# FFN chains in a two-layer hybrid decoder: where the addition, the scaled copy, the convolution taps and the gelu or gate product are issued

## The chip, the cores and the metric

The kernel runs on one core of one Trainium2 chip. The metric is the device time of one execution in microseconds, the median of three runs; it is compared with the same kernel after the change.

## The reference

A decoder trunk of two layers works on x of shape (1, 512, 1024) in float32. Layer 0 mixes tokens by dilated windowed attention, layer 1 by a gated recurrent block. Each is followed by a gated feed-forward block (FFN), and every block is wrapped in RMS norms. The change touches the FFN alone:

```python
D_FF = 3 * D_MODEL            # 3072

def causal_dwconv(x, w, b):   # K = 3 taps along the sequence
    xp = jnp.pad(x, ((0, 0), (K - 1, 0), (0, 0)))
    out = b
    for k in range(K):
        out = out + xp[:, k:k + S] * w[k]
    return out

def conv_ffn(x, w_up, conv_w, conv_b, w_down):
    u = causal_dwconv(x @ w_up, conv_w, conv_b)
    g, v = u[..., :D_FF], u[..., D_FF:]
    return (jax.nn.gelu(g, approximate=True) * v) @ w_down
```

## The kernel before

**Arithmetic.** Every matrix product is made of three passes of float32r matmuls: each operand is split into a high part (`whi`, a copy on ScalarE, line 149) and a low part (`wlo`, what the copy left out, a subtraction on VectorE, line 150). A weight of one unit can be multiplied only when both engines have split it.

**Chunks and chains.** The 6144 columns of `w_up` come in 12 chunks j of 256 gate columns (half 0) and 256 value columns (half 1). Chunks 0 to 2 are multiplied in the plain way. For chunks 3 to 11 (`SEVEN`) each half is a *chain*: seven products of 128x128x256 blocks in place of eight. The chain's steps are numbered 1 to 7 and collect in two PSUM banks: the *top* bank `y[0]` (output features 0 to 127) and the *bottom* bank `y[1]`. There are 18 chains in each layer; we call them c0 to c17, an even number for half 0 (gate) and an odd one for half 1 (value).

**Slots.** `seven` lays the steps on a line of slots, ten for each chain (`CYCLE`). Within a chain's ten, `AT` puts step 1 in slot 0, step 5 in 1, step 2 in 2, step 6 in 4, step 3 in 5, step 7 in 8, and step 4 in slot 3 of the next ten. Slots 6, 7 and in some chains 9 hold fill: quarters of the last plain chunk at first, then products of `w_down`'s first columns into four PSUM banks `acc` (line 412). Slots that hold nothing are skipped.

**What a slot issues.** `slot` emits the matmuls of its step, then counts down the list `due` and runs what has reached its turn, then `tick` splits one further unit of weights (line 149 on ScalarE, line 150 on VectorE). `later(0, f)` called from a step runs f at the end of the same slot, `later(1, f)` at the end of the next one; called from the list itself, f runs one slot later than that. Each engine works through its own instructions strictly in the order of issue, as written by this code; nothing rearranges them later.

**After the steps.** ScalarE copies three partial products out of PSUM (`part`, line 1032) before a later step adds to the same place. After step 3 comes the top's chain of work: the addition on VectorE (line 1036), the scaled copy on ScalarE with the middle tap's weight and the bias (line 773), the two other taps on VectorE, which read the bank once more (line 777), and at last either gelu on ScalarE (line 795, even chains) or the gate product on VectorE (line 799, odd chains). After step 7 VectorE adds a partial product to the bottom bank (line 1041), and step 4 adds to that bank in turn, so TensorE waits for line 1041. After step 4 the bottom has its scaled copy, taps, and gelu or gate product.

The waiting list stands in these lines:

```python
    def later(n, f):
        due.append([n, f])

    def slot(emit, length=1):
        emit()
        for d in list(due):
            d[0] -= 1
            if d[0] < 0:
                due.remove(d)
                d[1]()
        tick(length)
```

`begin` issues the scaled copy when it is called, puts the taps on the list with `later(0, taps)`, and returns gelu or the gate product for `finish` to put on the list.

Of the kernel before, what the change touches and what calls it, by code (L numbers as in the profile page):

```python
# [83 lines left out]
def kernel(  # L84
# [45 lines left out]
    def psum(s="ps"):  # L130
        return pp.tile([P, 512], F32, tag="ps", name=nm(s))
# [60 lines left out]
    def free_slots(n):  # L192

        end = CYCLE * n
        free = [CYCLE * c + r for c in range(n) for r in ((6, 7, 9) if c < 3 or c > 8 else (6, 7))][2:] + [end, end + 1]
        assert not {CYCLE * c + a for c in range(n) for a in AT.values()} & set(free)
        return free
# [149 lines left out]
    def take(i, j):  # L347
        while (i, j) not in units:
            before = state["live"]
            pump(1)  # L350
            assert before != state["live"], (i, j, state)
        return units[i, j]

    def done(n=2):
        state["live"] -= n
# [6 lines left out]
# [11 lines that stand above are left out]
# [37 lines left out]
    def mm3(dst, l, r, start, stop):  # L410
        for n, (a, b) in enumerate(PASSES):
            mm(dst, l[a], r[b], start=start and n == 0, stop=stop and n == 2)  # L412
# [569 lines left out]
    def rights(hT, T):  # L982

        def block(kr, n):
            return lambda h, k: hT[h][:, 4 * kr + k, n * 256 : n * 256 + 256]

        def turn(n):
            return lambda h, k: T[n][h][k // 2][:, k % 2]

        return {  # L990
            1: block(0, 0), 2: block(1, 0), 3: block(1, 1), 5: turn(0), 6: turn(1), 7: turn(2), 4: turn(3),
        }

    def quarters(i, m, hT, finish):
        ps = []

        def quarter(n):
            W = take(i, m)
            if not n:
                ps.append(psum())  # L1000
            for k in (2 * n, 2 * n + 1):
                mm3(ps[0], [w[k // 4][:, k % 4, :] for w in W], [h[:, k, :] for h in hT], k == 0, k == KD - 1)
            if n % 2:
                done(1)
            if n == 3:
                later(1, lambda: finish(ps[0]))

        return [lambda n=n: quarter(n) for n in range(4)]

    def chain(right, top, bottom):  # L1010

        i = chunk()
        y, t = {}, []

        def step(n):
            W = take(i, LEFT[n][0])
            b, at = {1: (1, 0), 6: (1, 0), 7: (1, 0), 4: (1, 0), 5: (0, 256), 3: (0, 256), 2: (0, 0)}[n]
            if b not in y:
                y[b] = psum()
            dst = y[b][:, at : at + 256]  # L1020
            for k in range(4):
                for q, (wa, ha) in enumerate(PASSES):
                    mm(  # L1023
                        dst, W[wa][0][:, k, :], right[n](ha, k), start=n in (1, 5) and k == q == 0,
                        stop=k == 3 and q == 2, skip_group_check=True,
                    )
            done(1)
            if n == 1:
                t.extend(gen(s="part") for _ in range(2))
            if n in (1, 5, 6):  # L1030
                to = {1: t[0][:, 0:256], 6: t[0][:, 256:512], 5: t[1][:, 0:256]}[n]
                later(1, lambda: nc.scalar.activation(to, dst, AF.Copy))  # L1032
            elif n == 3:

                def upper():
                    nc.vector.tensor_tensor(y[0], y[0], t[0], op=ALU.add)  # L1036
                    top(y[0])

                later(1, upper)
            elif n == 7:  # L1040
                later(1, lambda: nc.vector.tensor_tensor(y[1][:, 256:512], dst, t[1][:, 0:256], op=ALU.add))  # L1041
            elif n == 4:
                later(1, lambda: bottom(y[1]))

        return lambda n: lambda: step(n)

    def seven(hT, T, begin, last, prep):

        right = rights(hT, T)
        i0, acc, ends_at = state["next"], {}, CYCLE * 2 * len(SEVEN)  # L1050

        def finish(b, ps, j, minus=False):
            later(1, begin(b, ps, j, minus, True))

        def ends(j, half):
            return lambda ps: finish(2 * half, ps, j), lambda ps: finish(2 * half + 1, ps, j, True)

        def rows(k, pair):
            W, A = take(i0, ("rows", k)), take(i0, ("act", k))
            for t in pair:  # L1060
                if t not in acc:
                    acc[t] = psum("acc")
                mm3(acc[t], [a[0][:, t * P : (t + 1) * P] for a in A], [w[0] for w in W], not k, False)
            if pair[-1] == 3:
                done(2)

        fill = []
        for m in range(2):
            fill += quarters(last, m, hT, lambda ps, m=m: finish(2 + m, ps, SEVEN[0] - 1))
        fill += [lambda k=k, p=p: rows(k, p) for k in range(REST[0]) for p in ((0, 1), (2, 3))]  # L1070
        steps = {}
        n = 0
        for j in SEVEN:
            for half in range(2):
                f = chain(right, *ends(j, half))
                steps.update((CYCLE * n + AT[p], f(p)) for p in AT)
                n += 1
        free = free_slots(n)
        assert len(free) == len(fill)
        steps.update(zip(free, fill))  # L1080
        state["even"] = True
        for m in range(max(steps) + 1):
            if m == ends_at - 2:
                prep()
            if m in steps:
                slot(steps[m])
        while due:
            slot(lambda: None)
        done(2)
        state["even"] = False  # L1090
        return acc
# [626 lines left out]
```

## Time and profile before

| what | value |
|---|---|
| median of three runs (lowest to highest) | 1433.02 us (1432.54 to 1433.49) |
| profiled execution: its own time | 1433.17 us |
| profiled execution: span of the core | 1431.3 us |
| TensorE busy | 1407.8 us, 98% of the span |
| VectorE busy | 1124.2 us, 79% |
| ScalarE busy | 789.8 us, 55% |
| granted TensorE clock, mean | 0.999 |

The profile names engines PE (TensorE matmul), PEld (TensorE weight load), DVE (VectorE), ACT (ScalarE), POOL (GpSimd) and SP (SyncE). A row of the timeline begins with start and duration in microseconds; idle time of the engine just before it, and what ended that, stand in brackets at its end. The 18 chains of layer 0 lie between 549 and 805 us of the span, those of layer 1 between 1096 and 1352 us.

### The profile page before, as it was taken

Reading aid. Unit: us, or ns where it says so; the run is one execution under the profiler, and the core shown is the slowest. Engines: PE = TensorE matmul, PEld = TensorE weight load, DVE = VectorE, ACT = ScalarE, POOL = GpSimd, SP = SyncE. Lnnn points to the kernel's source line nnn. Section 1 sums busy time; section 2 is a strip of 40 time slices with the busy share of each in tenths; the row PEclk is TensorE's granted clock in tenths of the full one; section 3 lists DMA queues with packets and bytes.
Section 4 is the critical chain, followed back from the end, with each engine's and each line's share of the span. In section 5 each row is a group of like instructions: output and inputs, shape, how many; then the busy total and the mean of one; then the engine's idle time right before and its main releaser. Section 6 shows DMA issues by size and latency. Waiting matters only on the chain.

```text
span 1431.3 us, 23653 instructions
## 1 busy us (share of the span) xinstructions
PE 1407.8 (98%) x8741; PEld 1266.5 (88%) x8741; DVE 1124.2 (79%) x2201; ACT 789.8 (55%) x1646; POOL 225.3 (16%) x344
## 2 busy tenths in 40 slices
PE   9999999999999999999999999999999999999998
PEld 7888999999998888899999889888898989999886
DVE  6676898787855988888887758779789888888843
ACT  7343555363636555556656545588455656665641
POOL 0341333130400102121110001000102112111000
PEclk9999999999999999999999999999999999999999
DMA  7653455564756446576663632432345657574411
GB/s 225 180 145 106 131 166 153 169 181 141 196 165 220 164 131 127 112 155 149 132 151 86 221 118 89 133 118 89 118 151 107 154 112 157 135 151 117 165 64 60
DMA packets 171886, 201.93 MB, mean 141 GB/s; under 512 B 10561, under 2 KB 141081, under 8 KB 171513
## 3 DMA queue, kind: packets, MB, share of 16 engines
q1 hardware_dynamic: 123064, 153.34, 33.7%
q0 software_dynamic: 47856, 46.02, 17.6%
q8 instruction: 69, 1.13, 0.3%
q10 hardware_dynamic: 848, 1.05, 0.2%
q14 instruction: 49, 0.39, 0.1%
HBM read 181.41 MB, written 18.96 MB: 140 GB/s over the span
## 4 chain that ended last, share of the span: by engine, by line
PE 78%; DVE 12%; ACT 6%; issue 3%; DMA 1%; POOL 0%; DVEq 0%; SPq 0%; ACTq 0%
PE ps L1023 32%; PE acc L412 24%; PE ps L412 10%; PE v L1216 7%; DVE wlo L150 3%; DVE u L777 3%; ACT whi L149 2%; PE v L1154 1%; DVE xb L1521 1%; PE O L1428 1%; PE S L1362 1%; PE S L1310 1%; DVE T L150 1%; DVE u L799 1%; DVE B L939 1%
## 5 line engine op out<-in xcount | busy, mean ns | idle before, releaser
L150 DVE TENSOR_TENSOR wlo<-raw,whi 128x512 fp32r<-128x512 f32 x620 | 410.0, 687 | 130.5 <-ACT whi L149 125.8
L149 ACT ACTIVATE whi<-raw 128x512 fp32r<-128x512 f32 x620 | 366.6, 625 | 173.4 <-PE ps L1023 52.0
L1023 PE MATMUL ps<-T,whi 128*128 128x256 f32 x1664 | 305.3, 283 | 14.2 <-DVE ps L1041 10.5
L412 PE MATMUL ps<-hT,whi 128*128 128x512 f32 (+1 forms) x1088 | 288.0, 353 | 0.0
L1023 PEld LDWEIGHTS ps<-T,whi 128*128 128x128 f32 x1664 | 258.4, 189 | 21.7 <-DVE ps L1041 13.9
L1023 PE MATMUL ps<-T,wlo 128*128 128x256 f32 x832 | 232.9, 280 | 0.0
L1023 PE MATMUL ps<-hT,whi 128*128 128x256 f32 x1248 | 230.5, 283 | 0.0
L412 PEld LDWEIGHTS ps<-hT,whi 128*128 128x128 f32 x1088 | 190.8, 189 | 26.4
L1023 PEld LDWEIGHTS ps<-hT,whi 128*128 128x128 f32 x1248 | 195.7, 191 | 2.6
L412 PE MATMUL ps<-hT,wlo 128*128 128x512 f32 (+1 forms) x544 | 191.3, 352 | 0.0
L1023 PE MATMUL ps<-hT,wlo 128*128 128x256 f32 x624 | 176.4, 283 | 0.0
L186 POOL DMA_DIRECT2D raw<-in_ffn_w_up_dram x72 | 92.8, 1318 | 438.1 <-DVE wlo L150 294.5
L1023 PEld LDWEIGHTS ps<-T,wlo 128*128 128x128 f32 x832 | 158.1, 190 | 0.0
L412 PE MATMUL acc<-whi,ahi 128*128 128x512 f32 x352 | 137.6, 391 | 0.0
L412 PE MATMUL acc<-whi,alo 128*128 128x512 f32 x352 | 137.2, 390 | 0.2
L412 PE MATMUL acc<-wlo,ahi 128*128 128x512 f32 x352 | 137.0, 389 | 0.0
L1023 PEld LDWEIGHTS ps<-hT,wlo 128*128 128x128 f32 x624 | 119.3, 191 | 0.0
L412 PEld LDWEIGHTS ps<-hT,wlo 128*128 128x128 f32 x544 | 102.9, 189 | 14.0
L1216 PE MATMUL v<-whi,hT 128*128 128x512 f32 x320 | 106.5, 396 | 0.0
L777 DVE SCALAR_TENSOR_TENSOR u<-ps,cols,u 128x511 f32<-128x511 f32 x120 | 89.6, 747 | 5.0 <-ACT u L773 2.9
L773 ACT ACTIVATE u<-ps,cols 128x512 f32<-128x512 f32 x60 | 46.4, 774 | 76.8 <-DVE ps L1036 66.5
L1032 ACT ACTIVATE part<-ps 128x256 f32<-128x256 f32 x156 | 58.3, 374 | 50.0 <-PE ps L1023 49.1
(206 smaller groups left out, 2145.2 us busy)
## 6 DMA issues: line engine op xcount, KB each, us to landing
raw<-in_ffn_w_up_dram SPq DMA_DIRECT2D x48, 1024.0 KB
raw<-in_attn_w_qkv_dram SPq DMA_DIRECT2D x67, 512.0 KB
raw<-in_ffn_w_up_dram POOLq DMA_DIRECT2D x72, 256.0 KB, 5.7
raw<-in_ffn_w_down_dram SPq DMA_DIRECT2D x14, 1024.0 KB
dw<-in_ffn_w_down_dram SPq DMA_DIRECT2D x40, 256.0 KB
raw<-in_lru_w_in_dram SPq DMA_DIRECT2D x8, 1024.0 KB
turned<-T POOLq DMA_DIRECT2D x26, 256.0 KB, 2.6
ft<-turned POOLq DMA_DIRECT2D x104, 64.0 KB, 4.9
```

Source lines behind the costliest of these rows:

```text
L149: nc.scalar.activation(hi, raw, AF.Copy)
L150: nc.vector.tensor_tensor(lo, raw, hi.bitcast(F32), op=ALU.subtract)
L186: nc.gpsimd.dma_start(to, src, accum_op=ALU.add)
L412: mm(dst, l[a], r[b], start=start and n == 0, stop=stop and n == 2)
L773: nc.scalar.activation(u, ps, AF.Identity, scale=own[:, j : j + 1], bias=cc[:, 48 + j : 49 + j])
L777: nc.vector.scalar_tensor_tensor(u[:, d:], ps[:, : S - d], wc, u[:, d:], op0=ALU.mult, op1=ALU.add)
L799: nc.vector.tensor_tensor(g, g, u, op=ALU.mult)
L939: tt(o, hi.bitcast(F32), lo.bitcast(F32), op=ALU.add)
L1023: mm(dst, W[wa][0][:, k, :], right[n](ha, k), start=n in (1, 5) and k == q == 0, stop=k == 3 and q == 2, skip_group_check=True,)
L1032: later(1, lambda: nc.scalar.activation(to, dst, AF.Copy))
L1154: mm(banks[t], hT[a][:, k, t * P : (t + 1) * P], W[b][k % 2][:, 0, :], start=u == n == 0, stop=u == 3 and n == 5,)
L1216: mm(bank, hT[a][:, k, t * P : (t + 1) * P], W[b][k % 2][:, 0, :], start=(k, a, b) == (0, 0, 0), stop=(k, a, b) == (KD - 1, 1, 0),)
```

## The change

For the top bank, `ends` now puts the call of `finish` on the list with `later(0, ...)`, so the scaled copy is issued one slot after the addition in place of the same slot, and the taps one slot later too. `finish` puts gelu or the gate product three slots behind the scaled copy in place of two; this holds for tops, for bottoms, and for the two quarters of the last plain chunk, which end in `finish` too. No instruction is added or removed, and the matmuls keep their order.

```diff
         def finish(b, ps, j, minus=False):
-            later(1, begin(b, ps, j, minus, True))
+            later(2, begin(b, ps, j, minus, True))

         def ends(j, half):
-            return lambda ps: finish(2 * half, ps, j), lambda ps: finish(2 * half + 1, ps, j, True)
+            return (
+                lambda ps: later(0, lambda: finish(2 * half, ps, j)),
+                lambda ps: finish(2 * half + 1, ps, j, True),
+            )
```

How this moves instructions is seen in three pieces, all of layer 0. Names carry the number that the program gives a tile (`ps_7361` is chain c6's top bank, `ps_7335` its bottom bank); between the two programs these numbers shift by one or more without meaning.

First, VectorE in the even chain c6, from the split before the top's addition to the bottom's addition, before:

```order
L799 TENSOR_TENSOR u_7267<-u_7267,u_7426 128x512
L1036 TENSOR_TENSOR ps_7361<-ps_7361,part_7348 128x512
L150 TENSOR_TENSOR wlo_7462<-raw_7039,whi_7461 128x512
L777 SCALAR_TENSOR_TENSOR u_7459<-ps_7361,cols_1202,u_7459 128x511
L777 SCALAR_TENSOR_TENSOR u_7459<-ps_7361,cols_1202,u_7459 128x510
L150 TENSOR_TENSOR wlo_7474<-raw_7200,whi_7473 128x512
L150 TENSOR_TENSOR wlo_7491<-raw_7200,whi_7490 128x512
L1041 TENSOR_TENSOR ps_7335<-ps_7335,part_7349 128x256
```

And the same place after the change:

```order
L1036 TENSOR_TENSOR ps_7360<-ps_7360,part_7347 128x512
L150 TENSOR_TENSOR wlo_7459<-raw_7037,whi_7458 128x512
L799 TENSOR_TENSOR u_7267<-u_7267,u_7426 128x512
L150 TENSOR_TENSOR wlo_7472<-raw_7199,whi_7471 128x512
L777 SCALAR_TENSOR_TENSOR u_7469<-ps_7360,cols_1202,u_7469 128x511
L777 SCALAR_TENSOR_TENSOR u_7469<-ps_7360,cols_1202,u_7469 128x510
L150 TENSOR_TENSOR wlo_7490<-raw_7199,whi_7489 128x512
L1041 TENSOR_TENSOR ps_7334<-ps_7334,part_7348 128x256
```

The addition L1036 moved ahead of a gate product, and the taps moved behind one more split; L1041 keeps its place in the row.

Second, ScalarE at the same place in c6, from the split before the scaled copy to the copy of the next chain's step 1, before:

```order
L149 ACTIVATE whi_7447<-raw_7039 128x512
L773 ACTIVATE u_7459<-ps_7361,cols_1206 128x512
L149 ACTIVATE whi_7461<-raw_7039 128x512
L149 ACTIVATE whi_7473<-raw_7200 128x512
L795 ACTIVATE u_7459<-u_7459 128x512
L149 ACTIVATE whi_7490<-raw_7200 128x512
L149 ACTIVATE whi_7510<-raw_7039 128x512
L1032 ACTIVATE part_7507<-ps_7494 128x256
```

And after the change:

```order
L149 ACTIVATE whi_7447<-raw_7037 128x512
L149 ACTIVATE whi_7458<-raw_7037 128x512
L773 ACTIVATE u_7469<-ps_7360,cols_1206 128x512
L149 ACTIVATE whi_7471<-raw_7199 128x512
L149 ACTIVATE whi_7489<-raw_7199 128x512
L149 ACTIVATE whi_7509<-raw_7037 128x512
L795 ACTIVATE u_7469<-u_7469 128x512
L1032 ACTIVATE part_7506<-ps_7493 128x256
```

One split moved ahead of the scaled copy L773, and gelu L795 moved behind two more splits, to stand right in front of the `part` copy.

Third, VectorE in the chain c2, one of the first, where the fill is still quarters of the last plain chunk. Before:

```order
L799 TENSOR_TENSOR u_6603<-u_6603,u_6778 128x512
L1036 TENSOR_TENSOR ps_6711<-ps_6711,part_6702 128x512
L150 TENSOR_TENSOR wlo_6815<-raw_6572,whi_6814 128x512
L777 SCALAR_TENSOR_TENSOR u_6812<-ps_6711,cols_1202,u_6812 128x511
L777 SCALAR_TENSOR_TENSOR u_6812<-ps_6711,cols_1202,u_6812 128x510
L150 TENSOR_TENSOR wlo_6827<-raw_6572,whi_6826 128x512
L150 TENSOR_TENSOR wlo_6844<-raw_6443,whi_6843 128x512
L210 TENSOR_TENSOR raw_6572<-raw_6572 128x4x128
L1041 TENSOR_TENSOR ps_6689<-ps_6689,part_6703 128x256
```

And after the change:

```order
L1036 TENSOR_TENSOR ps_6711<-ps_6711,part_6701 128x512
L150 TENSOR_TENSOR wlo_6812<-raw_6572,whi_6811 128x512
L799 TENSOR_TENSOR u_6603<-u_6603,u_6778 128x512
L150 TENSOR_TENSOR wlo_6825<-raw_6572,whi_6824 128x512
L777 SCALAR_TENSOR_TENSOR u_6822<-ps_6711,cols_1202,u_6822 128x511
L777 SCALAR_TENSOR_TENSOR u_6822<-ps_6711,cols_1202,u_6822 128x510
L150 TENSOR_TENSOR wlo_6843<-raw_6443,whi_6842 128x512
L210 TENSOR_TENSOR raw_6572<-raw_6572 128x4x128
L1041 TENSOR_TENSOR ps_6688<-ps_6688,part_6702 128x256
```

Again the addition moved ahead of the gate product, and the taps behind one more split. In c3, which follows, two gate products that stood ahead of L1041 now stand behind it.

## The prediction

> **What bounds the kernel now.** I read the page first, then who waited for whom on TensorE in the two FFN stretches, then the timeline of each wait found, then VectorE and ScalarE ahead of it. The page's first part says that TensorE sets the time:
>
> ```profile
> PE 1407.8 (98%) x8741; PEld 1266.5 (88%) x8741; DVE 1124.2 (79%) x2201; ACT 789.8 (55%) x1646; POOL 225.3 (16%) x344
> ```
>
> VectorE and ScalarE matter only where TensorE waits for them. In the chains of layer 0 (549 to 805 us) the view of waits has just two rows for TensorE, with total, count and longest; for layer 1 (1096 to 1352 us) it gives the same two rows with the same numbers:
>
> ```profile
> PE ps L1023 <- DVE ps L1041: 4.7, 5, 1.6
> PE ps L1023 <- ACT part L1032: 1.8, 1, 1.8
> ```
>
> So a layer has five stalls on the bottom's addition (L1041) and one on a `part` copy. That one stands at the start of chain c0, ahead of the first instruction that the change moves, and stays. Four of the five in TensorE's timeline (the missing one is at 620.88 us); the bracket holds the idle time:
>
> ```profile
> 592.92 0.50 PE L1023 MATMUL ps<-T,whi 128*128 128x256 f32 x2 [1.60 <-DVE ps L1041]
> ...
> 607.30 0.51 PE L1023 MATMUL ps<-T,whi 128*128 128x256 f32 x2 [1.38 <-DVE ps L1041]
> ...
> 647.26 0.50 PE L1023 MATMUL ps<-T,whi 128*128 128x256 f32 x2 [0.58 <-DVE ps L1041]
> ...
> 673.66 0.50 PE L1023 MATMUL ps<-T,whi 128*128 128x256 f32 x2 [0.58 <-DVE ps L1041]
> ```
>
> Each is step 4 of a chain: at 592.92 that of c2, then c3, (c4), c6 and c8. How long TensorE needs where nothing holds it is seen in the chain of waits (start, duration, what):
>
> ```profile
> 592.92 4.55 PE ps L1023 x36
> ...
> 712.03 8.58 PE ps L1023 x72
> 720.61 2.75 PE acc L412 x12
> 723.36 1.42 PE ps L1023 x12
> ...
> 799.59 1.70 PE ps L1023 x12
> ```
>
> A step of 12 matmuls takes 8.58 / 6 = 1.43 us; six steps, two fills and step 7 make a cycle of 8.58 + 2.75 + 1.42 = 12.75 us. After a stall three steps take 4.55 where 3 x 1.43 = 4.29 would do: each stall costs 0.26 us more than its idle time.
>
> Why is L1041 late? VectorE in c6, then ScalarE in the same stretch:
>
> ```profile
> 639.44 0.68 DVE L150 TENSOR_TENSOR wlo<-raw,whi 128x512 fp32r<-128x512 f32 x1
> 640.04 0.68 DVE L799 TENSOR_TENSOR u<-u,u 128x512 f32<-128x512 f32 x1
> 640.64 0.69 DVE L1036 TENSOR_TENSOR ps<-ps,part 128x512 f32<-128x512 f32 x1
> 642.76 0.69 DVE L150 TENSOR_TENSOR wlo<-raw,whi 128x512 fp32r<-128x512 f32 x1 [1.42 <-ACT whi L149]
> 643.37 1.53 DVE L777 SCALAR_TENSOR_TENSOR u<-ps,cols,u 128x511 f32<-128x511 f32 x2
> 644.81 0.68 DVE L150 TENSOR_TENSOR wlo<-raw,whi 128x512 fp32r<-128x512 f32 x1
> 646.17 0.69 DVE L150 TENSOR_TENSOR wlo<-raw,whi 128x512 fp32r<-128x512 f32 x1 [0.68 <-ACT whi L149]
> 646.78 0.43 DVE L1041 TENSOR_TENSOR ps<-ps,part 128x256 f32<-128x256 f32 x1
> ```
>
> ```profile
> 641.43 0.78 ACT L773 ACTIVATE u<-ps,cols 128x512 f32<-128x512 f32 x1 [2.59 <-DVE ps L1036]
> 642.11 1.14 ACT L149 ACTIVATE whi<-raw 128x512 fp32r<-128x512 f32 x2
> 644.99 0.63 ACT L795 ACTIVATE u<-u 128x512 f32<-128x512 f32 x1 [1.74 <-DVE u L777]
> 645.53 1.13 ACT L149 ACTIVATE whi<-raw 128x512 fp32r<-128x512 f32 x2
> 646.57 0.36 ACT L1032 ACTIVATE part<-ps 128x256 f32<-128x256 f32 x1
> ```
>
> The two engines block each other. ScalarE stands 2.59 us in front of the scaled copy, which needs the addition, with splits queued behind it; VectorE then waits 1.42 us for such a split. ScalarE next stands 1.74 us in front of gelu, which needs the taps, and VectorE waits 0.68 us for the split behind it. Those 2.10 us in the row ahead of L1041 are more than the 0.58 us by which L1041 is late.
>
> **The change part by part.** Nothing is added or removed; no DMA and no matmul is moved against its own engine's order. What changes is which instruction stands at the head of a queue when its input is not there.
>
> *Even chain, c6.* Instructions on VectorE start 0.60 to 0.61 us apart (639.44, 640.04, 640.64), two taps take 1.44 (643.37 to 644.81). In the new row the addition takes the gate product's place at 640.04. The scaled copy starts 0.79 later (641.43 less 640.64), at 640.83; the split behind it 0.68 later, at 641.51, and its `wlo` 0.65 later (642.76 less 642.11), at 642.16. Meanwhile VectorE has a `wlo` whose split is now ahead of the scaled copy, in ScalarE's 2.59 idle us (640.64), and the gate product (641.24 to 641.84): it idles 0.32, not 1.42. Then `wlo` 642.16, taps 642.77, `wlo` 644.21 (its split followed at 642.1), L1041 at 644.82, over at 645.25. TensorE asks at 647.26 - 0.58 = 646.68. Margin 1.4 us, with nothing gained earlier; c8 has the same rows.
>
> *c2.* VectorE, with ScalarE's copy behind it:
>
> ```profile
> 585.16 0.69 DVE L799 TENSOR_TENSOR u<-u,u 128x512 f32<-128x512 f32 x1
> 585.76 0.69 DVE L1036 TENSOR_TENSOR ps<-ps,part 128x512 f32<-128x512 f32 x1
> 587.82 0.69 DVE L150 TENSOR_TENSOR wlo<-raw,whi 128x512 fp32r<-128x512 f32 x1 [1.36 <-ACT whi L149]
> ...
> 592.45 0.43 DVE L1041 TENSOR_TENSOR ps<-ps,part 128x256 f32<-128x256 f32 x1
> ```
>
> ```profile
> 586.49 0.78 ACT L773 ACTIVATE u<-ps,cols 128x512 f32<-128x512 f32 x1 [4.97 <-DVE ps L1036]
> ```
>
> New: addition 585.16, `wlo` 585.76, gate product 586.36, copy 585.89 (0.73 behind the addition), split 586.57, its `wlo` 587.22, taps 587.83, `wlo` 589.27, L210 589.87, L1041 590.48 to 590.91. TensorE asks at 592.92 - 1.60 = 591.32: margin 0.4 us, the smallest; what c0 and c1 save in the same way would come on top.
>
> *c3.* Two gate products leave the row ahead of L1041:
>
> ```profile
> 601.39 0.69 DVE L150 TENSOR_TENSOR wlo<-raw,whi 128x512 fp32r<-128x512 f32 x1 [1.43 <-ACT whi L149]
> ...
> 606.82 0.43 DVE L1041 TENSOR_TENSOR ps<-ps,part 128x256 f32<-128x256 f32 x1
> ```
>
> L1041 was at 606.82; c2's gain of 1.97, two gate products (1.2) and the idle 1.43 (the first split now stands ahead of the copy, and the quarter's taps come before the top's) put it at 602.2 to 602.7. TensorE, 1.86 us earlier by c2's stall, asks at 607.30 - 1.38 - 1.86 = 604.06: margin 1.4. The two gate products then delay c4 by 1.2, and c4 saves 1.8 of its own idle time as c6 does; its margin comes out near 1.3.
>
> *Odd chains.* They have no stall; there the gate product moves from ahead of L1041 to behind it, 0.6 us in favour. In c17 L1041 came so late that step 4 took 1.70 us (at 799.59) in place of 1.42: 0.28 comes back.
>
> *What gets later.* The top's bank is emptied one split (0.6 us) later in the row. By the Trainium skill (PSUM — Partial Sum Buffer, Summary: rules for kernel authors) a bank should be emptied promptly, PSUM being tight; that speaks against the change. The trace has no TensorE wait for L777 at all, so here I set it at nothing; it is a rival below. Gelu and gate products come up to three units later, and their products are read in fills and in the down projection, chains later.
>
> *Sum.* Per layer 4.7 (the idle time of the five stalls, by the row of the waits; the four that are shown make 4.14 of it) + 5 x 0.26 + 0.28 = 6.3; both layers 12.6 us. A second way: from 592.92 to 673.66 lie 80.74 us and six cycles of 12.75 = 76.5, so 4.24, with the first 1.60 and 0.28 makes 6.12, both layers 12.2 us. I take 12.4. The profiled execution's own time is 1433.17, 0.15 above the median of 1433.02; from the median, **1420.6 us**. Bounds: the 0.26 terms don't come back (10.0 us saved, 1423), or the whole first sum does, on a run at the low end of those shown (1432.54 - 12.6 = 1419.9).
>
> **The rivals.** *A, half the gain.* c2's 0.4 us is thin: if ScalarE's splits there are held by something else than the scaled copy, c2 and c3 keep stalling and only the three small stalls go: 2 x (4.7 - 1.60 - 1.38 + 3 x 0.26) = 5.0 us, 1428. For it: ScalarE's 4.97 us at c2's copy say that VectorE was far behind by its own work. Against: in those 4.97 us ScalarE could have made the splits that VectorE then waits for. Chance 0.12.
>
> *B, slower: gelu in front of the `part` copy.* In even chains the copy of the next chain's step 1 now stands right behind gelu, and gelu waits for the taps. Step 6 adds where that copy reads. In c6 the new taps end at 644.21, gelu and copy (0.63 + 0.36) at 645.3; step 6 is one step behind step 4, at 646.68 + 1.43 = 648.1. It decides once taps end after 647.1, 2.9 us later than worked out. If TensorE then waited 1 us in each of the 18 even chains, 18 x 1.26 = 22.7 lost against 12.4 gained: 1443. For it: gelu did wait 1.74 us for the taps in c6. Against: the margin. Chance 0.04.
>
> *C, slower: the bank.* A chain that takes over a top's bank waits for its taps. c6's taps end at 644.81, and c7 already writes both its banks:
>
> ```profile
> 643.66 0.40 PE L1023 MATMUL ps<-T,whi 128*128 128x256 f32 x2
> ```
>
> So the taker is c8 at the earliest, a cycle later, and a move of 0.6 us does not reach it. If it did, one step of 1.43 in 36 chains would give 51 us, about 1472. This is what the skill's rule above would lead to; chance 0.01.
>
> *D, no change.* TensorE runs into another wait of the same size at the same step, a split that is itself paced by a buffer TensorE frees. Against it: no TensorE wait for a split stands in the two rows above. About 1433; chance 0.03.
>
> **How the numbers follow.** The forecast has 0.80: 1419.5 to 1423. With A at 0.12 near 1428 and values between (c2's stall left: 1420.6 + 2 x 1.86 = 1424), the range 1419 to 1427 leaves out most of A and B, C and D, under 2 in 10. A measurement of this kernel can tell about 0.2%, 2.9 us, from no change. Forecast and A are faster by more: 0.92; D 0.03 within; slower B and C, 0.05.
>
> **What would show it.** Right: TensorE's waits for L1041 in the two stretches gone, cycles c3 to c8 12.75 us long, VectorE's wait ahead of the split behind the scaled copy near 0.3 us in even chains, ScalarE's waits at L773 well below the 2.59 and 4.97 us of before. c2 alone still stalling means the margin there was misjudged. Wrong: waits for L1032 in even chains (B), for L777 (C), or for L150 (D).

## The result

| what | before | after |
|---|---|---|
| median of three runs (lowest to highest) | 1433.02 us (1432.54 to 1433.49) | 1420.84 us (1420.83 to 1420.89) |
| ratio after / before, 95% interval | | 0.9915 [0.9893, 0.9938] |
| profiled execution: own time, span | 1433.17, 1431.3 us | 1420.89, 1419.1 us |
| granted TensorE clock, mean | 0.999 | 0.998 |

The changed kernel is 12.2 us faster; 1420.6 was forecast.

### The profile page after: what moved, and what is told of

It reads as the page before. It is cut to its first block, busy times and chain, and to the rows that moved or that the text cites. A ratio compares the mean times of both kernels' runs of the same rounds, so it can differ in the third digit from the quotient of the medians.

```text
span 1419.1 us, 23634 instructions
## 1 busy us (share of the span) xinstructions
PE 1406.0 (99%) x8741; PEld 1267.6 (89%) x8741; DVE 1125.1 (79%) x2201; ACT 800.6 (56%) x1646; POOL 225.8 (16%) x344
## 4 chain that ended last, share of the span: by engine, by line
PE 83%; DVE 9%; ACT 5%; issue 1%; DMA 0%; POOL 0%; DVEq 0%; ACTq 0%
PE ps L1023 35%; PE acc L412 25%; PE ps L412 11%; PE v L1219 7%; DVE wlo L150 3%; DVE u L777 2%; PE v L1157 1%; DVE xb L1524 1%; PE O L1431 1%; PE S L1365 1%; ACT whi L149 1%; PE S L1313 1%; DVE T L150 1%; DVE B L939 1%; ACT sig L1545 1%
## 5 line engine op out<-in xcount | busy, mean ns | idle before, releaser
L149 ACT ACTIVATE whi<-raw 128x512 fp32r<-128x512 f32 x620 | 371.0, 626 | 189.3 <-PE ps L1023 76.3
L1023 PE MATMUL ps<-T,whi 128*128 128x256 f32 x1664 | 304.3, 283 | 4.2 <-ACT part L1032 3.5
L1023 PEld LDWEIGHTS ps<-T,whi 128*128 128x128 f32 x1664 | 259.3, 190 | 8.9 <-ACT part L1032 3.9
L1023 PE MATMUL ps<-T,wlo 128*128 128x256 f32 x832 | 233.3, 280 | 0.0
L1023 PE MATMUL ps<-hT,whi 128*128 128x256 f32 x1248 | 231.4, 284 | 0.0
L1023 PEld LDWEIGHTS ps<-hT,whi 128*128 128x128 f32 x1248 | 196.6, 192 | 2.6
L1023 PE MATMUL ps<-hT,wlo 128*128 128x256 f32 x624 | 176.8, 283 | 0.0
L1023 PEld LDWEIGHTS ps<-T,wlo 128*128 128x128 f32 x832 | 158.4, 190 | 0.0
L1023 PEld LDWEIGHTS ps<-hT,wlo 128*128 128x128 f32 x624 | 119.8, 192 | 0.0
L1032 ACT ACTIVATE part<-ps 128x256 f32<-128x256 f32 x156 | 58.7, 376 | 71.7 <-PE ps L1023 68.7
L777 DVE SCALAR_TENSOR_TENSOR u<-ps,cols,u 128x511 f32<-128x511 f32 x120 | 89.4, 746 | 5.0 <-ACT u L773 2.9
L412 PEld LDWEIGHTS acc<-whi,alo 128*128 128x128 f32 x352 | 66.1, 188 | 14.9 <-DVE alo L150 1.1
```

The source lines that it names most:

```text
L149: nc.scalar.activation(hi, raw, AF.Copy)
L777: nc.vector.scalar_tensor_tensor(u[:, d:], ps[:, : S - d], wc, u[:, d:], op0=ALU.mult, op1=ALU.add)
L1023: mm(dst, W[wa][0][:, k, :], right[n](ha, k), start=n in (1, 5) and k == q == 0, stop=k == 3 and q == 2, skip_group_check=True,)
```

## The profile after

The first part of the page of the changed kernel: every engine runs as many instructions as before. ScalarE is busy for 10.8 us more; instructions that start apart overlap less (below, two splits apart take 0.62 and 0.63 us, where two in a row took 1.14).

```profile
PE 1406.0 (99%) x8741; PEld 1267.6 (89%) x8741; DVE 1125.1 (79%) x2201; ACT 800.6 (56%) x1646; POOL 225.8 (16%) x344
```

Who waited for whom on TensorE in the whole run of the changed kernel (total, count, longest). Below line 1060 its line numbers are 3 higher than before.

```profile
PE ps L1023 <- ACT part L1032: 3.5, 2, 1.8
PE warm L1640 <- DVE one L1685: 1.5, 1, 1.5
PE ps L1023 <- DVE ps L1041: 0.7, 1, 0.7
```

The `part` copy at c0 is the only wait left in the two FFN stretches, once per layer. The one on L1041 lies outside them. The ten stalls on L1041 are gone.

VectorE in c6 of the changed kernel, then ScalarE there (start, duration, idle time in the bracket):

```profile
636.66 0.69 DVE L1036 TENSOR_TENSOR ps<-ps,part 128x512 f32<-128x512 f32 x1
637.26 0.68 DVE L150 TENSOR_TENSOR wlo<-raw,whi 128x512 fp32r<-128x512 f32 x1
637.86 0.68 DVE L799 TENSOR_TENSOR u<-u,u 128x512 f32<-128x512 f32 x1
638.72 0.69 DVE L150 TENSOR_TENSOR wlo<-raw,whi 128x512 fp32r<-128x512 f32 x1 [0.18 <-ACT whi L149]
639.33 1.53 DVE L777 SCALAR_TENSOR_TENSOR u<-ps,cols,u 128x511 f32<-128x511 f32 x2
640.77 0.68 DVE L150 TENSOR_TENSOR wlo<-raw,whi 128x512 fp32r<-128x512 f32 x1
641.37 0.43 DVE L1041 TENSOR_TENSOR ps<-ps,part 128x256 f32<-128x256 f32 x1
```

```profile
637.39 0.78 ACT L773 ACTIVATE u<-ps,cols 128x512 f32<-128x512 f32 x1 [0.70 <-DVE ps L1036]
638.07 0.62 ACT L149 ACTIVATE whi<-raw 128x512 fp32r<-128x512 f32 x1
638.94 0.63 ACT L149 ACTIVATE whi<-raw 128x512 fp32r<-128x512 f32 x1 [0.26 <-PE ps L1023]
640.37 0.64 ACT L149 ACTIVATE whi<-raw 128x512 fp32r<-128x512 f32 x1 [0.79 <-PE ps L1023]
640.95 0.63 ACT L795 ACTIVATE u<-u 128x512 f32<-128x512 f32 x1
641.49 0.36 ACT L1032 ACTIVATE part<-ps 128x256 f32<-128x256 f32 x1
```

Before, VectorE idled 1.42 and 0.68 us in this row; now 0.18. ScalarE waited 2.59 us at the scaled copy and 1.74 at gelu; now 0.70 and nothing. Two of its three splits here are now released by TensorE (`<-PE ps L1023`): in c6 the two engines hardly hold each other up, and run at TensorE's pace. In c2 ScalarE still stands 2.47 us at the copy and 1.75 at gelu (layer 1), and this does no harm: ahead of each now stands a split that VectorE can go on with, and VectorE idles 0.17 us where it idled 1.36 and 0.68. In c6, L1041 ends at 641.80, and TensorE comes to step 4 later, without a bracket:

```profile
643.14 0.40 PE L1023 MATMUL ps<-T,whi 128*128 128x256 f32 x2
```

The chain of waits of the changed kernel (start, duration, what): in each layer the row behind c0's stall, which begins with c0's step 6, two cycles of layer 0, and the two rows that close the chains of a layer.

```profile
552.36 6.05 PE ps L1023 x36
...
609.38 2.75 PE acc L412 x12
612.12 9.99 PE ps L1023 x84
622.12 2.75 PE acc L412 x12
624.87 9.99 PE ps L1023 x84
...
794.42 1.43 PE ps L1023 x12
795.85 43.67 PE acc L412 x192
...
1094.03 4.53 PE ps L1023 x36
...
1336.00 76.30 PE acc L412 x336
```

A cycle takes 2.75 + 9.99 = 12.74 us without a break, as forecast, and step 4 of c17, 1.70 before, takes 1.43. Something is new too: the three steps behind c0's stall take 6.05 us in layer 0, where they take 4.53 in layer 1 and took 4.53 in both layers before.

The row behind c0's stall and the row behind the last chain's step 4 bound a stretch that we call the chains; it gives their own gain. These are the four rows of the chain of waits before:

```profile
552.87 4.53 PE ps L1023 x36
...
801.29 3.43 PE acc L412 x15
...
1099.60 4.53 PE ps L1023 x36
...
1348.03 3.43 PE acc L412 x15
```

| stretch | before | after | gained |
|---|---|---|---|
| start to c0's step 6 in layer 0 | 552.87 | 552.36 | 0.51 |
| chains of layer 0 (to 801.29, 795.85) | 248.42 | 243.49 | 4.93 |
| down projection and layer 1 to its c0's step 6 (to 1099.60, 1094.03) | 298.31 | 298.18 | 0.13 |
| chains of layer 1 (to 1348.03, 1336.00) | 248.43 | 241.97 | 6.46 |
| rest (to the span's end) | 83.27 | 83.10 | 0.17 |

Layer 1 gained 6.46 us, where the sum had 6.3. Layer 0 gained 1.53 less, which is what its longer row lost: 6.05 - 4.53 = 1.52.

## The experiments

The theory: ScalarE and VectorE block each other at the heads of their queues, first at the scaled copy, then at gelu; both edits let a split go first. The kernel before was measured again beside them: it took 1433.05 us beside the two edits taken singly and the two edits that go on top of the change, and 1433.38 beside the other three runs.

**Only the top moves.** `finish` stays as before:

```diff
         def finish(b, ps, j, minus=False):
             later(1, begin(b, ps, j, minus, True))

         def ends(j, half):
-            return lambda ps: finish(2 * half, ps, j), lambda ps: finish(2 * half + 1, ps, j, True)
+            return (
+                lambda ps: later(0, lambda: finish(2 * half, ps, j)),
+                lambda ps: finish(2 * half + 1, ps, j, True),
+            )
```

> The later scaled copy of the tops alone; gelu and gate product stay two slots behind the copy, so every gate product stays ahead of the addition or of L1041 as before. Theory (the two engines' blocking of each other is what made L1041 late; one of the two waits gone is enough): in c6 the addition stays at 640.64, the split behind the copy comes at 642.11 and its wlo at 642.76, but one wlo is done before it, so L1041 comes at 645.4 in place of 646.78, ahead of 646.68 when TensorE asks; c2 and c3 come out with margins of 0 to 0.3 us. 1421 to 1422.5, TensorE's waits for L1041 in the two stretches 0 to 1 us in all. Rival (what counts is that gate products no longer stand ahead of the addition and of L1041): nothing comes back, 1432 to 1433.

Measured: 1421.63 us (1421.54 to 1422.75), ratio 0.9921 [0.9907, 0.9934]. Nearly the whole gain, as expected. In either layer TensorE has only the wait at c0. Both rows behind that wait are slow ones here, so TensorE comes to c2 1.5 us later; whether c2 would stall without that, no trace shows. VectorE in c2 of this kernel:

```profile
585.55 0.69 DVE L1036 TENSOR_TENSOR ps<-ps,part 128x512 f32<-128x512 f32 x1
586.15 0.68 DVE L150 TENSOR_TENSOR wlo<-raw,whi 128x512 fp32r<-128x512 f32 x1
587.61 0.69 DVE L150 TENSOR_TENSOR wlo<-raw,whi 128x512 fp32r<-128x512 f32 x1 [0.77 <-ACT whi L149]
```

The work that stands ahead of L1041 on VectorE is what it was, and one split ahead of the copy is enough: VectorE waits 0.77 where it waited 1.36, and has a `wlo` to do meanwhile.

**Only the products move.** `finish` with `later(2, ...)`, `ends` as before:

```diff
         def finish(b, ps, j, minus=False):
-            later(1, begin(b, ps, j, minus, True))
+            later(2, begin(b, ps, j, minus, True))
```

> Gelu and gate product one slot later alone; the scaled copy stays in the slot of the addition. Theory: ScalarE still stands in front of the copy with splits behind it (1.4 us of VectorE's waiting per chain stay), but the second wait, 0.68 us, goes and the gate product leaves the row ahead of the addition: in c6 L1041 ends at 646.4 against 646.68, so c4, c6 and c8 stop stalling; c2 is about even, c3 (one gate product still ahead of L1041, the wait of 1.43 us too) stalls by some 0.5 us. 1421.5 to 1424. Rival (gate products alone count): 1421, the same as with both edits.

Measured: 1425.05 us, ratio 0.9944 [0.9931, 0.9956]: 8.0 us of the 12.2, and 1 us above the range that was expected. TensorE's timeline in layer 0 shows where, c4 among them, which had not been expected:

```profile
591.47 0.50 PE L1023 MATMUL ps<-T,whi 128*128 128x256 f32 x2 [0.30 <-DVE ps L1041]
...
605.11 0.50 PE L1023 MATMUL ps<-T,whi 128*128 128x256 f32 x2 [0.65 <-DVE ps L1041]
...
618.28 0.50 PE L1023 MATMUL ps<-T,whi 128*128 128x256 f32 x2 [0.17 <-DVE ps L1041]
```

So either edit alone brings most of the gain, 11.4 and 8.0; together they bring 12.2, not 19.4. Each works on the same lateness of L1041, and what is past the point at which TensorE asks is worth nothing.

**The products, parted.** First only gelu is moved, then only the gate products:

```diff
-            later(1, begin(b, ps, j, minus, True))
+            later(2 if b < 2 else 1, begin(b, ps, j, minus, True))    # gelu alone
+            later(1 if b < 2 else 2, begin(b, ps, j, minus, True))    # gate products alone
```

> Before, with only gelu (b below 2) three slots behind its scaled copy; gate products and tops as before. The kernel with both moved stood at 1425.05 us against 1433.05. Theory (the two engines block each other at the heads of their queues): gelu no longer stands in front of a split, which takes VectorE's 0.68 us wait out of the row ahead of L1041 in c2, c4, c6 and c8; the three late by 0.58 us or less stop stalling (3 x about 0.85 with the restart), c2 keeps about 0.9 us of its 1.60, c3 most of its 1.38, since its two gate products stay ahead of L1041. Per layer 3.1 to 3.8 us, 1425.5 to 1427. Rival (what counts is VectorE's own work ahead of L1041, so the gate products): 1431 to 1433, the stalls at c4, c6 and c8 still there.

> Before, with only the gate products (b of 2 or more) three slots behind; gelu and tops as before. Theory: the blocking stays, so the stalls at c2, c4, c6 and c8 stay near 1.6 and 0.6 us; only c3 gains, by the two gate products of 0.6 us that leave the row ahead of its L1041, and c4 gets part of that back: 1429.5 to 1432.5. Rival (VectorE's own work counts): most of the 8.0 us, 1425 to 1427.

Measured: gelu alone 1427.23 us (1425.62 to 1427.63), ratio 0.9956 [0.9943, 0.9968]; gate products alone 1432.75, ratio 0.9998 [0.9989, 1.0007], no gain that can be told. Both lie some 0.2 us above the ranges that were expected, and both profiles have a slow row behind c0's stall in layer 0. Layer 1 is free of it: its chains, 248.43 us before, take 244.82 with gelu alone and 248.01 with the gate products alone. That is 3.6 and 0.4 us per layer, and 244.42, or 4.0, with both. Blocking counts, and the work that stands ahead of L1041 does little. TensorE's timeline in layer 1, with gelu alone:

```profile
1136.03 0.51 PE L1023 MATMUL ps<-T,whi 128*128 128x256 f32 x2 [0.31 <-DVE ps L1041]
...
1150.41 0.50 PE L1023 MATMUL ps<-T,whi 128*128 128x256 f32 x2 [1.38 <-DVE ps L1041]
```

and with the gate products alone:

```profile
1139.56 0.51 PE L1023 MATMUL ps<-T,whi 128*128 128x256 f32 x2 [1.59 <-DVE ps L1041]
...
1153.21 0.50 PE L1023 MATMUL ps<-T,whi 128*128 128x256 f32 x2 [0.65 <-DVE ps L1041]
...
1167.15 0.50 PE L1023 MATMUL ps<-T,whi 128*128 128x256 f32 x2 [0.95 <-DVE ps L1041]
...
1193.52 0.51 PE L1023 MATMUL ps<-T,whi 128*128 128x256 f32 x2 [0.59 <-DVE ps L1041]
```

Gelu alone clears c4, c6 and c8, takes c2 from 1.60 to 0.31, where 0.9 was expected, and leaves c3 at 1.38. The gate products alone take c3 from 1.38 to 0.65 and hand 0.36 of that on to c4, which goes from 0.59 to 0.95; c2, c6 and c8 stay.

**The top's bank, deeper.** The changed kernel with its top three slots later still:

```diff
-                lambda ps: later(0, lambda: finish(2 * half, ps, j)),
+                lambda ps: later(3, lambda: finish(2 * half, ps, j)),
```

> The changed kernel with the scaled copy of the tops three slots later still, so that the taps empty the top bank some four us later than in the changed kernel, and the copy, no longer gelu, stands in front of the part copies. Theory: the addition is long done when ScalarE reaches the copy, banks are enough for a whole further chain, L1041 loses two taps ahead of it: no TensorE wait comes, 1420 to 1421.5, the same as the changed kernel. Rival (a bank that is emptied late holds up the chain that takes it over): waits of TensorE's first step of a chain for L777, one step of 1.43 us in up to 36 chains, up to 1472.

Measured: 1420.91 us (1419.63 to 1422.78), ratio 0.9915 [0.9901, 0.9929], and no wait for L777. The chains of layer 1 take 1336.23 - 1094.26 = 241.97 us, as in the changed kernel, though c6's taps start at 643.48 us in place of 639.33. When the top's bank is emptied does not matter here, even three slots later than the change puts it.

**The stall that is left.** The last plain tile's gelu, which stands ahead of c0's `part` copies on ScalarE, is put behind them (on top of the change):

```diff
+        def behind(ps, b, j):
+            later(3, begin(b, ps, j))
...
-        tiles(SEVEN[0] - 1, chunk(), (0, 1))
+        i = chunk()
+        feat_tile(i, 0, hT, lambda ps: begin(0, ps, SEVEN[0] - 1))
+        feat_tile(i, 1, hT, lambda ps: behind(ps, 1, SEVEN[0] - 1))
```

> The changed kernel with one thing more: gelu of the last plain tile ahead of the chains is put behind the part copies of chain c0's steps 1 and 5. Theory: the one stall left, 1.77 us in each layer, is a part copy queued behind that gelu, which waits for taps; the copy then comes at about 550.5 in place of 551.94, TensorE's wait shrinks to 0.3 us or less, so 1.5 + 0.26 us come back in each layer, 3.5 in all; if the half clock of three us behind that stall in layer 0 was set off by the idle time, 1.5 us more: 1415.8 to 1417.5. Rival (the stall is really VectorE's lateness at this place, gelu only the last in the row): another wait, for L1041 or for a split, takes its place, 1420 to 1421.

Measured: 1416.58 us (1416.3 to 1417.23), ratio 0.9883 [0.9868, 0.9898], the fastest kernel here, 4.3 us below the changed one. Its chain of waits, the row behind c0's stall in each layer, without a long one:

```profile
551.68 4.54 PE ps L1028 x36
...
1090.26 4.54 PE ps L1028 x36
```

The idle time ahead of c0's step 6 falls from 1.77 to 0.27 and 0.28: 2 x 1.5 = 3.0 us, and the 1.5 of layer 0's long row make 4.5. Nothing behind it takes this back: the chains take 241.98 us in both layers.

**The same edit without the change**, in the kernel before:

> Before, with only the last plain tile's gelu put on the list with later(3), so that it stands behind the part copies of c0's steps 1 and 5. On top of the change this edit was worth 4.3 us (1420.84 to 1416.58). Theory: VectorE between 550 and 592 us waits for nothing but ScalarE's splits (5.5 us in five waits), so its row does not move when TensorE is let go earlier; the 1.5 us that c0's stall loses comes back as a longer wait on L1041 in c2 (1.6 becomes 2.4 to 3.2 us), and the time stays within 1431.5 to 1433.3. Rival (stalls of a chain are independent terms that add up): 1428.5 to 1429.5, with c2's wait at 1.6 as before.

Measured: 1433.31 us (1431.63 to 1434.78), ratio 0.9997 [0.9989, 1.0006]. No gain that can be told, where on top of the change it was worth 4.3 us. TensorE's timeline in layer 0:

```profile
551.58 0.50 PE L1028 MATMUL ps<-T,whi 128*128 128x256 f32 x2 [0.27 <-ACT part L1037]
...
592.59 0.50 PE L1028 MATMUL ps<-T,whi 128*128 128x256 f32 x2 [2.14 <-DVE ps L1046]
```

c0's stall is gone (L1037 and L1046 are L1032 and L1041 of the other kernels), and TensorE starts 552.87 - 551.58 = 1.29 us earlier, but leaves c2's stall only 592.92 - 592.59 = 0.33 earlier: VectorE's row hardly followed. Of the difference, 0.42 us was lost ahead of c2, and c2 waits 2.14 in place of 1.60. The wait so made was itself followed by three slow steps (the next part), in both layers of this profile:

```profile
592.59 6.05 PE ps L1028 x36
```

It is the slowest of the eleven runs. Their time follows the granted clock: the four at a mean of 0.999 took 1431.63 to 1432.83 us, the kernel before at that mean 1432.90 to 1433.35. So some 1.2 us is kept where no such loss comes (an estimate from the mean clocks). The theory holds in direction: c2's wait, expected at 2.4 to 3.2 us, came out shorter, and the median lies at the upper end of its range. Independent terms that add up would have left c2's wait at 1.6; they are out.

## Why the prediction was right

- **The cause.** Right: the blocking at the scaled copy and at gelu. Letting a split go ahead of the copy brings 11.4 us by itself, letting splits go ahead of gelu 6.2 (1433.38 - 1427.23; 2 x 3.6 = 7.2 where no slow row comes in), moving only gate products nothing that can be told. The prediction did not say how far the two edits overlap.
- **The five stalls per layer.** Right, all gone. Rival A, with c2 and c3 still stalling, is out. The line that odd chains have no stall leaves out c3, an odd chain, whose stall the prediction counts apart.
- **c6's walk.** VectorE's wait was put at 0.32 and measures 0.18; L1041's margin, put at 1.4, is 643.14 - 641.80 = 1.34.
- **c2's margin.** Put at 0.4 us, it was too small: in layer 1 L1041 starts at 1130.31 and TensorE at 1132.33, so the margin is 1132.33 - 1130.74 = 1.6. From the addition to L1041's end the walk was exact (590.91 - 585.16 = 5.75 us; measured 1130.74 - 1124.99 = 5.75). What it had wrong was the addition's start: c2 was walked by itself, and what c0 and c1 save was named and not counted. Counted from c0's step 6, the addition starts after 1124.99 - 1094.03 = 30.96 us, where the walk had 585.16 - 552.87 = 32.29.

```profile
1130.31 0.43 DVE L1041 TENSOR_TENSOR ps<-ps,part 128x256 f32<-128x256 f32 x1
```

```profile
1132.33 0.40 PE L1023 MATMUL ps<-T,whi 128*128 128x256 f32 x2
```

- **The sum.** 6.3 per layer was forecast. Layer 1 gave 6.46, and with layer 0's long row corrected (4.93 + 1.52 = 6.45) both agree. That the total, 12.2, comes so near the 12.4 is in part luck: two things that the prediction did not have nearly cancel, 1.5 us lost behind c0's stall and 0.8 gained outside the chains (0.51 + 0.13 + 0.17). The 0.51 ahead of c0's step 6 stands already at a wait outside the FFN, which ends at 210.85 us before and at 210.34 after; from there both take 342.02 us to c0's step 6. The programs do the same work up to that wait, and in the nine profiles it ends anywhere from 210.34 to 211.18, so this is scatter.
- **Rivals B, C and D.** No wait for L1032 in a later chain than c0, none for L777, none for a split in the two stretches. C is refuted by the deeper top as well: the rule of the Trainium skill to empty banks promptly (PSUM — Partial Sum Buffer, Summary: rules for kernel authors) costs nothing that can be told when it is broken by a few slots in this kernel.

## What the hardware showed that had not been expected

After c0's stall the clock fell, though the mean over the run hides it. The stretches of 1 us in the changed kernel (the column with the decimal ahead of the DMA share is the granted clock):

```profile
552.00:553.00 1.00, 0.64 (x5) 0.64 (x6) 0.83 (x2) 1.00 (x5) 0.00 (x0) 1.00 1.22 151
553.00:554.00 1.00, 1.00 (x8) 1.00 (x8) 0.90 (x2) 1.00 (x3) 0.00 (x0) 0.60 1.17 145
554.00:555.00 1.00, 1.00 (x6) 1.00 (x6) 1.00 (x3) 0.48 (x3) 0.00 (x0) 0.50 0.07 8
555.00:556.00 1.00, 1.00 (x7) 1.00 (x6) 0.91 (x2) 1.00 (x3) 0.16 (x1) 0.50 0.41 110
556.00:557.00 1.00, 1.00 (x8) 1.00 (x8) 0.94 (x2) 0.13 (x1) 1.00 (x1) 0.69 0.96 301
557.00:558.00 1.00, 1.00 (x10) 1.00 (x10) 0.98 (x2) 0.24 (x1) 0.12 (x1) 1.00 1.09 387
```

The clock that is missing in these rows adds up to 0.40 + 0.50 + 0.50 + 0.31 = 1.71 us, so half clock lasted 1.71 / 0.5 = 3.4 us; in every other case below it comes to 3.4 us too. Three steps take 6.05 in place of 4.53. In the nine profiles, an idle time of 1.76 to 1.79 us was followed by this in 6 of 14 cases (in the kernel before in neither layer), one of 2.13 or 2.14 in 2 of 2, and one of 1.60 or less never. Between single runs of the deeper top it shows as steps of about 1.5 us: 1419.63 at a mean clock of 0.999, 1420.77 and 1421.04 at 0.998, 1422.78 at 0.996. What decides between equal stalls was not tried. The Trainium skill (TensorE: Matmul & The Clock Gate, Why this matters for your kernels) warns of idle gaps above about 3 us; here 1.8 us was enough at times. That its window runs free of the program (Part 1) would agree with a chance that differs from run to run; the runs show no more of it than the same 3.4 us of half clock each time.

Whether such a loss counts depends on what follows. In the kernel with the gate products alone the long row stood in layer 0 as well, and c2's stall behind it was 0.88 us where layer 1 had 1.59: the wait took in part of it. In the changed kernel no later stall takes it in.

## What to carry to other kernels

Where two engines feed each other through queues that run in order, look for an instruction that waits at the head of one while the other engine needs what stands behind it; putting ready work ahead of it is worth the bound engine's stall and no more. Stalls in a row are not terms that add up: where the next stall is set by another engine, a stall removed ahead of it hands most of its time to that one (the same edit was worth 4.3 us on top of this change, and nothing that can be told without it, where 0.33 of 1.29 us was left at c2), so remove first the one whose engine falls behind on its own. And a stall costs more than its idle time where the clock falls behind it.
